# Addresses of the gated values and order of the passes in the second products of two feed-forwards

## The chip, the core and the metric

The kernel runs on one core of a Trainium2 chip. The metric is device time in microseconds (us), the median of several executions. Instructions run on TensorE (PE in the profile; its weight loads are listed apart as PEld), VectorE (DVE), ScalarE (ACT), GpSimd (POOL) and SyncE (SP, which issues DMAs). SBUF is the on-chip memory with 128 partitions; PSUM holds the results of matmuls in eight banks.

## The reference

One decoder layer on 512 tokens of width 1024, all in float32: a feed-forward, a token mixer and a second feed-forward, each between norms. The change is inside both feed-forwards, in the product with `w_out`:

```python
D_MODEL = 1024
SEQ = 512
D_FF = 2816

def rms_norm(x, g):
    xf = x.astype(jnp.float32)
    y = xf * lax.rsqrt(jnp.mean(xf * xf, axis=-1, keepdims=True) + EPS)
    return (y * g.astype(jnp.float32)).astype(x.dtype)

def swiglu_ffn(x, w_in, w_out):
    gate, up = jnp.split(x @ w_in, 2, axis=-1)
    return (jax.nn.silu(gate) * up) @ w_out

def reference(...):
    for l in range(DEPTH):
        x = x + 0.5 * rms_norm(swiglu_ffn(rms_norm(x, norm_pre[l, 0]), ffn1_w_in[l], ffn1_w_out[l]),
                               norm_post[l, 0])
        mixed = token_mixer(rms_norm(x, norm_pre[l, 1]), ...)
        x = x + rms_norm(mixed, norm_post[l, 1])
        x = x + 0.5 * rms_norm(swiglu_ffn(rms_norm(x, norm_pre[l, 2]), ffn2_w_in[l], ffn2_w_out[l]),
                               norm_post[l, 2])
    return x
```

`jax.nn.silu(gate) * up`, 512 tokens by 2816, are the gated values; their product with `w_out` (2816 by 1024) is the second product of a feed-forward.

## The kernel before

**Three passes.** Every large product is made of float32r matmuls. A float32 operand is kept as two parts: high, the value cast to float32r, and low, the rest. A product is three passes, high by high, high by low, low by high, summed in PSUM. Each matmul has its own weight load: 128 by 128 stationary values are loaded, then 256 columns of the moving operand stream past them.

**First products** (`prod`, L504 on, matmul at L520) multiply by `w_in`: weights stationary, the activations moving. They are written pass by pass: for one pass, eight matmuls (two halves of the output by four pieces of the sum), then the next pass. `p1` to `p7` and `c1` to `e4` are the names of the products of one step. `left` says which buffer a product's activations lie in: `xq` (four tiles) or `sq` (three). `p7` reads `sq[1]`, whose high and low parts lie at different offsets mod 128 elements. The first products of the head have copies of the weights in the `sq` buffers (`stay`).

**Second products** (`ffn_out`) multiply the gated values by `w_out`: the gated values are stationary, 128 tokens by 128, and the weights move, 256 columns of a tile `w` at a time. The 1024 columns are done in two halves of 512. In each half a loop goes over the eleven gated tiles `k2` (256 values of the 2816 each) in the order `OUT`; in the second half it goes over seven of them, and the last four tiles are left for `chunk`, which finishes one block of 128 tokens after the other so that the norm of a block (`post1`, `after`) can begin while the next is multiplied (`last`, L436 on). Four accumulators `C`, one PSUM bank each, hold the results: `C[i % 2][v]` for token block `i` and column quarter `v`.

Most tiles are plain (`plain`, matmul at L778): 48 matmuls for four token blocks, two column quarters, two pieces `kk` and three passes. The passes are the innermost loop, so that a matmul by the high part of a weight is followed by the same stationary values by its low part. The tiles in `QUARTERED` (four in the first half, three in the second) use seven products instead of eight of a 2 by 2 block product (`quartered` and `product`, matmul at L786): 42 matmuls. Their operands are quarters of the gated tile (`h_quarters`) and sums of them (`h_sums`), and four more accumulators `M` are turned into terms `T` by `common` and added to `C` by `add` (L754). The quarters `kept` in the first half are read again in the second.

**Where the operands lie.** The weights are split into high and low by ScalarE (cast, L220) and VectorE (subtraction, L222) into one of four slots of the tile `w`, each of 2048 elements. A slot is given back by `drop`, and the split of the next weight tile into it waits for the last matmul that reads it. The gated tiles are split by `two_parts` (L713 and L714) into buffers of tag `s` (three, shared with `sq`) or into the tiles `xq`, which are free by then. `s_place` and `x_place` choose the offset inside them: `NEXT` is 16 elements, 64 bytes, and the low part follows the high one by 1024 elements, in the sums of quarters by 1024 + 112. One buffer starts at byte 224 mod 512, a tile `xq` at 160, a slot of `w` at 480 (some slots of the mixer's weights at 416).

**What orders the work.** Most of the program is written in source order, and a scheduler orders each engine's queue when the kernel is built: it may put a ready instruction of lower priority ahead of one whose inputs come later. `more` makes gated tiles ahead of their use; `feed` splits weights ahead as far as slots are free. At the end of the first feed-forward `head4` begins the mixer's products (L475) with the slots that `chunk` gives back.

## Time and profile before

| What | Value |
|---|---|
| median of three runs | 958.07 us (958.02 to 958.52) |
| the profiled execution | 960.42 us |
| its span, first to last instruction | 958.7 us |
| mean granted clock of TensorE | 0.997 |
| second products of the first feed-forward | 225.7 to 349.5 us of the span |
| second products of the second feed-forward | 830.9 to 952.5 us of the span |
| matmuls at L520, L778, L786 | 3744, 1440, 588 |

The page gives for each engine its busy time, for each group of instructions (line, engine, operation, operands, shape, count) its busy time and the mean duration of one, then the idle time of the engine just before them. A matmul's duration of some 280 ns is longer than the distance between the starts of two, because they overlap in the array: the pitch from start to start is what adds up to time. The chain of waits follows the work that ended last back from the end; a row gives start, length, engine, line and count. The timeline merges neighbouring instructions of one line and one set of tiles into a row.

### The profile page before, as it was taken

The page shows a single profiled execution, that of the slowest core. Times are in us where ns is not written, and L with a number is a line of the kernel's source. Part 1 is how long each engine was busy: PE and PEld are TensorE (multiplying, and loading weights), DVE is VectorE, ACT ScalarE, POOL GpSimd, SP SyncE. Part 2 cuts the span into 40 slices and gives each one's busy share as a digit, 9 for nine tenths or more (in the row PEclk, how much of TensorE's full clock was granted, in tenths as well). Part 3 has the DMA queues.
Part 4 walks back from the last instruction along what each step waited for, and adds up shares of the span by engine and source line. Part 5 has one row for each costly group of instructions (what it writes and reads, how often), then busy time and mean ns, then how long its engine had stood idle before and what let it go on. Part 6 is the DMA issues. An engine that isn't in the chain of part 4 may idle for free.

```text
span 958.7 us, 18146 instructions
## 1 busy us (share of the span) xinstructions
PE 949.0 (99%) x7531; PEld 915.4 (95%) x7531; DVE 775.2 (81%) x1052; ACT 489.5 (51%) x691; POOL 119.1 (12%) x177
## 2 busy tenths in 40 slices
PE   9999999999999999999999999999999999999997
PEld 7999999999999999998887888899999999999997
DVE  6799989999788776688846565697998899977883
ACT  7645444455445456955622444664444444644541
POOL 2430000000001045200001210353000000000101
PEclk9999999999999999999999999999999999999999
DMA  9244343244232024421222124324334333224212
GB/s 320 77 134 130 116 128 111 89 133 131 87 96 84 23 78 123 111 66 44 70 64 67 45 80 139 112 67 133 111 110 121 111 110 101 66 89 133 73 39 88
DMA packets 81677, 96.13 MB, mean 100 GB/s; under 512 B 4117, under 2 KB 61497, under 8 KB 81594
## 3 DMA queue, kind: packets, MB, share of 16 engines
q1 hardware_dynamic: 81306, 94.44, 32.1%
q8 instruction: 59, 0.97, 0.4%
q10 hardware_dynamic: 288, 0.52, 0.2%
q14 instruction: 24, 0.20, 0.1%
HBM read 92.85 MB, written 2.10 MB: 99 GB/s over the span
## 4 chain that ended last, share of the span: by engine, by line
PE 62%; DVE 1%; ACT 0%; POOL 0%; issue 0%; POOLq 0%; DVEq 0%; ACTq 0%
PE ps L520 22%; PE ps L778 9%; PE ps L465 6%; PE ps L136 5%; PE ps L138 5%; PE ps L137 5%; PE ps L786 4%; PE ps L1163 2%; PE ps L475 1%; PE ps L295 1%; PE ps L1337 0%; PE ps L1248 0%; PE ps L1444 0%; PE ps L1417 0%; PE ps L1203 0%; PE ps L1441 0%
## 5 line engine op out<-in xcount | busy, mean ns | idle before, releaser
L220 ACT CAST w<-raw 128x1024 fp32r<-128x1024 f32 (+1 forms) x228 | 235.6, 1039 | 260.5 <-PE ps L520 94.5
L222 DVE TENSOR_TENSOR w<-raw,w 128x1024 fp32r<-128x1024 f32 (+1 forms) x228 | 281.9, 1243 | 46.9 <-ACT w L220 46.7
L520 PE MATMUL ps<-xq,w 128*128 128x256 f32 x2016 | 238.0, 277 | 0.0
L520 PEld LDWEIGHTS ps<-xq,w 128*128 128x128 f32 x2016 | 233.4, 188 | 0.0
L520 PE MATMUL ps<-sq,w 128*128 128x256 f32 x1440 | 171.0, 277 | 0.0
L520 PEld LDWEIGHTS ps<-sq,w 128*128 128x128 f32 x1440 | 167.4, 188 | 0.0
L778 PE MATMUL ps<-w,hs 128*128 128x256 f32 x1344 | 163.2, 281 | 0.0
L778 PEld LDWEIGHTS ps<-w,hs 128*128 128x128 f32 x1344 | 159.9, 189 | 0.3
L236 DVE TENSOR_TENSOR raw<-raw,raw 128x1024 f32<-128x1024 f32 x64 | 80.2, 1253 | 0.6
L136 PE MATMUL ps<-w,xq 128*128 128x512 f32 x192 | 79.0, 412 | 0.1
L138 PE MATMUL ps<-w,xq 128*128 128x512 f32 x192 | 75.0, 392 | 0.0
L137 PE MATMUL ps<-w,xq 128*128 128x512 f32 x192 | 74.9, 391 | 0.0
L383 POOL TENSOR_SCALAR col<-col 128x1 f32<-128x1 f32 x24 | 9.6, 401 | 500.9 <-ACT junk L382 500.8
L465 PE MATMUL ps<-xq,w 128*128 128x256 f32 x480 | 58.1, 283 | 0.0
L465 PEld LDWEIGHTS ps<-xq,w 128*128 128x128 f32 x480 | 56.9, 189 | 0.5 <-issue 0.5
L236 POOL TENSOR_TENSOR raw<-raw,raw 128x1024 f32<-128x1024 f32 x16 | 43.1, 2695 | 51.2 <-DVE w L222 42.0
L136 PEld LDWEIGHTS ps<-w,xq 128*128 128x128 f32 x192 | 36.1, 188 | 8.2 <-issue 0.8
L138 PEld LDWEIGHTS ps<-w,xq 128*128 128x128 f32 x192 | 36.1, 188 | 8.2 <-DVE xq L302 0.3
L137 PEld LDWEIGHTS ps<-w,xq 128*128 128x128 f32 x192 | 36.2, 189 | 6.7 <-issue 0.2
L713 ACT CAST hs<-hf 128x1024 fp32r<-128x1024 f32 x28 | 29.3, 1047 | 24.9 <-PE ps L786 24.9
L786 PE MATMUL ps<-w,hs 128*128 128x256 f32 x336 | 41.9, 282 | 0.0
L786 PEld LDWEIGHTS ps<-w,hs 128*128 128x128 f32 x336 | 40.6, 189 | 0.0
(251 smaller groups left out, 1151.8 us busy)
## 6 DMA issues: line engine op xcount, KB each, us to landing
raw<-in_ffn_w_in_dram SPq DMA_DIRECT2D x88, 512.0 KB, 3.8
raw<-in_ffn_w_out_dram SPq DMA_DIRECT2D x44, 512.0 KB, 4.0
raw<-in_w_mix_in_dram SPq DMA_DIRECT2D x28, 512.0 KB, 3.8
raw<-in_w_mix_out_dram SPq DMA_DIRECT2D x8, 512.0 KB, 3.9
out_dram<-xs SPq DMA_DIRECT2D x8, 256.0 KB, 2.1
xs<-in_x_dram SPq DMA_DIRECT2D x6, 256.0 KB, 6.8
gpost<-in_norm_post_dram SPq DMA_DIRECT2D x3, 512.0 KB
gpre<-in_norm_pre_dram SPq DMA_DIRECT2D x2, 512.0 KB, 4.1
```

What stands on the lines that cost most here:

```text
L136: mm(ps, sh, mh, start=start, stop=False, **kw)
L137: mm(ps, sh, ml, start=False, stop=False, **kw)
L138: mm(ps, sl, mh, start=False, stop=stop, **kw)
L220: nc.scalar.copy(hi, raw)
L222: nc.vector.tensor_tensor(lo, raw, hi.bitcast(F32), op=ALU.subtract)
L236: (nc.vector if late else nc.gpsimd).tensor_tensor(o, o, c, op=ALU.add)
L465: mm(ps[:, u0:u1], w[:, a, k, :], self.xop(k, b, u0, u1), start=k + n + m == 0, stop=k == ND - 1 and n == 2, skip_group_check=True,)
L520: self.nc.tensor.matmul(ps[:, c], wb[b][:, k, v], left[d][:, k, :], start=first and a + n + k == 0, stop=n == 2 and k == KH - 1, skip_grou ...
L713: self.nc.scalar.copy(hi, src)
L778: mm(out, a[kk][:, i * P : (i + 1) * P], w[:, b, kk, QUARTER * v : QUARTER * (v + 1)], start=begin and c == kk == n == 0, stop=kk == 1 and ...
L786: mm(ps[:, QUARTER * c : QUARTER * (c + 1)], A[a][:, c], B[b], start=begin and c == n == 0, stop=n == 2, skip_group_check=True,)
L1163: nc.tensor.matmul(sc[:, 64 * m : 64 * m + 64], k8[:, m], q8[:, m], start=True, stop=True)
```

## The change

Three things are altered, all in `ffn_out` and the helpers that place its operands.

The gated values of each feed-forward (`layer` 0 or 1) and each half of the columns get offsets of their own, in elements: (16, 0), (64, 64), (80, 80) and (96, 96) for the high and the low part, mod 128 elements, that is mod 512 bytes. With the buffers as they lie, the high and low parts start at bytes 288 and 224, 480 and 480, 32 and 32, 96 and 96 mod 512. The quarters kept from the first half stay where that half put them.

The matmuls of a plain tile are grouped: for two of the four token blocks, eight matmuls of the first pass, then eight of the second, then eight of the third; then the other two token blocks. Those of a quartered tile are grouped for each of its two weights: six and eight to a pass. In the last four tiles a group is one token block and one column quarter over all four tiles, eight matmuls to a pass.

The four weight slots of the last tiles are given back at the end of the last token block; the program between has no split.

```diff
-RAW, WBUF, PAD, LATE, NEAR, NEXT = 3, 4, 128, 112, 48, 16
+RAW, WBUF, PAD, LATE, NEAR = 3, 4, 128, 112, 48
...
+LIES = [[(16, 0), (64, 64)], [(80, 80), (96, 96)]]
...
-    def s_place(self, a=2, apart=False):
+    def s_place(self, lies, a=2):
 
         t = self.hpool.tile([P, 2 * D + PAD], F32R, tag="s", bufs=3, name=self.nm("hs"))
         part = lambda o: t[:, o : o + D].rearrange("p (k t) -> p k t", k=a)
-        return part(NEXT), part(D + (PAD if apart else NEXT))
-
-    def x_place(self, *n):
+        return part(lies[0]), part(lies[0] + D + (lies[1] - lies[0]) % PAD)
+
+    def x_place(self, lies, *n):
 
         out = []
         for m in range(2):
             t = self.xq[n[m % len(n)]].rearrange("p b k t -> p (b k t)")
-            o = 2 * NEXT + (D * m if len(n) == 1 else 0)
+            o = PAD - LATE + lies[m] + (D * m if len(n) == 1 else 0)
             out.append(t[:, o : min(o + D, 2 * D)])
         return out
...
+        def passes(group):
+
+            for n, (a, b) in enumerate(((0, 0), (0, 1), (1, 0))):
+                for out, left, right, first, last in group:
+                    mm(out, left[a], right[b], start=first and n == 0, stop=last and n == 2, skip_group_check=True)
 
         def plain(C, w, h, i, v, begin):
...
             for kk in range(2):
-                for n, (a, b) in enumerate(((hi, 0), (hi, 1), (lo, 0))):
-                    mm(
-                        out, a[kk][:, i * P : (i + 1) * P], w[:, b, kk, QUARTER * v : QUARTER * (v + 1)],
-                        start=begin and c == kk == n == 0, stop=kk == 1 and n == 2, skip_group_check=True,
-                    )
+                left = [t[kk][:, i * P : (i + 1) * P] for t in (hi, lo)]
+                right = [w[:, b, kk, QUARTER * v : QUARTER * (v + 1)] for b in range(2)]
+                yield out, left, right, begin and c == kk == 0, kk == 1
...
             w = self.pull()
-            product(M["p1"], A(1), quarter(w, 1), begin)
-            product(C[1][1], A(3), quarter(w, 3), False)
-            product(C[1][0], S(3), quarter(w, 2), False)
+            group = [*product(M["p1"], A(1), quarter(w, 1), begin), *product(C[1][1], A(3), quarter(w, 3), False)]
+            passes([*group, *product(C[1][0], S(3), quarter(w, 2), False)])
             self.drop(w)
             v = self.pull()
-            product(M["p7"], S(0), quarter(v, 0), begin)
-            product(M["p5"], S(1), quarter(v, 1), begin)
-            product(M["p6"], S(2), quarter(v, 2), begin)
-            product(C[0][1], A(2), quarter(v, 3), False)
+            group = [*product(M["p7"], S(0), quarter(v, 0), begin), *product(M["p5"], S(1), quarter(v, 1), begin)]
+            group += product(M["p6"], S(2), quarter(v, 2), begin)
+            passes([*group, *product(C[0][1], A(2), quarter(v, 3), False)])
             self.drop(v)
...
                     w = self.pull()
                     more(n + 3)
-                    for i in (0, 2, 1, 3):
-                        for v in range(2):
-                            plain(C, w, h, i, v, m == 0)
-                        if i > 1 and T and (half or m == PAIRS - 1):
-                            add(C, T, i % 2)
+                    for u in range(2):
+                        passes([mm for i in (u, u + 2) for v in range(2) for mm in plain(C, w, h, i, v, m == 0)])
+                        if T and (half or m == PAIRS - 1):
+                            add(C, T, u)
                     self.drop(w)
...
         def chunk(i):
             for v in range(2):
-                for w, h in zip(ws, hs):
-                    plain(C, w, h, i, v, False)
-                    if v and i == NT - 1:
-                        self.drop(w)
+                passes([mm for w, h in zip(ws, hs) for mm in plain(C, w, h, i, v, False)])
                 yield 2 - v
+            if i == NT - 1:
+                for w in ws:
+                    self.drop(w)
```

`product` now yields the same five values as `plain`, and `h_tile`, `h_quarters` and `h_sums` hand on the offsets of the half they are called for; `self.layer` counts the feed-forwards.

More of the change, by code (lines that the diff above doesn't have):

```diff
@@ L721, in h_tile, with h_quarters @@
         return hi, lo
-    def h_quarters(self, k2, n):
+    def h_quarters(self, k2, n, lies):
         src = self.by_chunk(k2)
-        parts = [v[:, : 3 * QUARTER].rearrange("p (k c t) -> p k c t", c=2, t=P) for v in self.x_place(n)]
+        parts = [v[:, : 3 * QUARTER].rearrange("p (k c t) -> p k c t", c=2, t=P) for v in self.x_place(lies, n)]
         self.two_parts(*(v[:, 0] for v in parts), src[:, 0, 1])
@@ L733, in by_chunk, with h_sums @@
         return self.hf[:, 2 * k2 : 2 * k2 + 2, :].rearrange("p k (c u t) -> p k u c t", u=2, t=P)
-    def h_sums(self, k2):
+    def h_sums(self, k2, lies):
         nc = self.nc
@@ L762, in more @@
                 half, k2 = seq[count[0]]
+                lies = LIES[self.layer][half]
                 count[0] += 1
@@ L765, in more @@
                     if half == 0:
-                        kept[k2] = self.h_quarters(k2, (1, 2, 0, 3)[QUARTERED[0].index(k2)])
-                    made.append((kept[k2], self.h_sums(k2)))
-                else:
-                    made.append((self.h_tile(k2, self.x_place(2, 3) if count[0] == len(seq) else None), None))
+                        kept[k2] = self.h_quarters(k2, (1, 2, 0, 3)[QUARTERED[0].index(k2)], lies)
+                    made.append((kept[k2], self.h_sums(k2, lies)))
+                else:
+                    made.append((self.h_tile(k2, self.x_place(lies, 2, 3) if count[0] == len(seq) else self.s_place(lies)), None))
+        def passes(group):
+            for n, (a, b) in enumerate(((0, 0), (0, 1), (1, 0))):
+                for out, left, right, first, last in group:
+                    mm(out, left[a], right[b], start=first and n == 0, stop=last and n == 2, skip_group_check=True)
         def plain(C, w, h, i, v, begin):
```

13 lines of the change are left out of this document (5 added, 8 removed).

## The prediction

> **What bounds the kernel.** I read the page first: busy times, groups, then the waits of the tensor engine.
>
> ```profile
> span 958.7 us, 18146 instructions
> PE 949.0 (99%) x7531; PEld 915.4 (95%) x7531; DVE 775.2 (81%) x1052; ACT 489.5 (51%) x691; POOL 119.1 (12%) x177
> L778 PE MATMUL ps<-w,hs 128*128 128x256 f32 x1344 | 163.2, 281 | 0.0
> L786 PE MATMUL ps<-w,hs 128*128 128x256 f32 x336 | 41.9, 282 | 0.0
> ```
>
> TensorE is busy 99% of the span, and the view of its waits adds up to 3.2 us, none of them at the changed lines L778 and L786. So the time there is the number of matmuls times their pitch (start to start), and nothing else ends last. The change keeps every matmul; only the pitch and the order can move the time. The granted clock is 0.997 over the run and 1.00 in these stages, so a pitch that differs is not the clock.
>
> The pitch shows in the chain of waits for the second feed-forward, whose columns are start, length, line and count:
>
> ```profile
> 830.88 5.65 PE ps L778 x48
> 836.53 2.74 PE ps L520 x24
> 839.27 5.65 PE ps L778 x48
> 844.92 4.95 PE ps L786 x42
> ...
> 933.14 18.93 PE ps L778 x167
> ```
>
> A plain block of 48 takes 5.65 us, 117.7 ns each; a quartered one 4.95/42 = 117.9. The 24 matmuls of L520 between them, of the same size, take 114.2, and 167 of the last matmuls of L778, in the same order as the slow ones, 113.4. So there are two paces, 113.3 and 117.8, and the second products run nearly all at the slow one: a matmul's start and the next weight load lock to each other in one of two ways.
>
> What selects the pace shows in the first products, by the timeline of TensorE (start, length, line, tiles, count):
>
> ```profile
> 630.69 2.99 PE L520 MATMUL ps<-xq,w 128*128 128x256 f32 x24
> 633.52 5.83 PE L520 MATMUL ps<-xq,sq 128*128 128x256 f32 x48
> 639.18 8.64 PE L520 MATMUL ps<-xq,w 128*128 128x256 f32 x72
> 647.66 2.99 PE L520 MATMUL ps<-xq,sq 128*128 128x256 f32 x24
> 650.49 2.99 PE L520 MATMUL ps<-xq,w 128*128 128x256 f32 x24
> 653.32 3.00 PE L520 MATMUL ps<-sq,w 128*128 128x256 f32 x24
> 656.15 2.88 PE L520 MATMUL ps<-xq,w 128*128 128x256 f32 x24
> 658.87 5.38 PE L520 MATMUL ps<-sq,w 128*128 128x256 f32 x46
> ```
>
> I divide the difference of starts by the count (a row's length has the last matmul's drain in it). Let the distance be the moving operand's start minus the start of the next stationary one, in bytes mod 512; the addresses are those of the built kernel before (w at 480, the buffers s at 224, xq at 160). With w stationary L520 has a distance of 192. Its rows at 630.69, 639.18 and 650.49 run at 117.8 to 117.9, the one at 656.15 and most that follow at 113.3, all in the same pass by pass order: so distance 192 bears both paces. The product between them, p7 at 653.32, has its low part at another address: passes of eight at 192, 192 (high part) and 256 (low part). In its records the eight at 256 are 120 apart, and after them the pace is the quick one. In every later p7 the eight at 256 average 117.6, the next eight 115.8, the next eight 113.3, so p7 means 115.5. Distance 448 (xq moving, sq stationary) also bears both paces: 113.3 from 621.8 to 624.3, 117.8 at 647.66. Where the low part of the stationary makes it 256 inside those products, eight matmuls run at a flat 120, in four places. Distance 384 occurs at a few: once each time L520 hands over to L778, where the matmul takes 117 to 118, the next few 114 to 119, and the pace is slow from there (four of four), and in four matmuls of L1248 (118, 120, 119, 118; its load is 100 wide). Distance 0 occurs only as the single matmul ahead of each L520 behind L778: 117, then 121 and 122. So I take odd multiples of 64 (192, 448) as bearing either pace, and even ones (0, 256, 384) as held at about 120.
>
> **Part by part.** Each feed-forward has 504 matmuls in the first half of the columns (7 plain blocks of 48, 4 quartered of 42), 318 in the loop of the second (4 and 3), and 192 in its last four tiles. Before, all gated parts are at distance 192, but for the low sums at 256. After:
>
> 1. First feed-forward, first half, (16, 0): 192 for passes one and two, 256 for pass three, eight and eight and eight: p7's pattern. 504 x (115.5 - 117.8) = -1.2 us. Bounds: 113.3 throughout, -2.3; never kicked to the quick pace, (2 x 117.8 + 120)/3 = 118.5, +0.4. I take p7's row, the nearest.
> 2. First feed-forward, second half, (64, 64): distance 0. In the loop 192 plain and 72 with sums, 264 in all, go from 117.8 to 120: +0.6; the 54 that read the quarters kept from the first half stay, 0. The last tiles now average 114.6 (186 records, without six with stalls), so 186 x (120 - 114.6) = +1.0. Together +1.6. Bounds: at 113.3, -1.4; at 125, the highest single pitch at a change of distance, +3.8.
> 3. Second feed-forward, first half, (80, 80): 448, either pace, entered from L520 through a single matmul at 128, which no row shows; the nearest, 384, led to the slow pace each time. So 0; at 113.3 it is -2.3; at most +0.1.
> 4. Second feed-forward, second half, (96, 96): 384. Loop 264 x 2.2 = +0.6; the last tiles lose the quick pace: 167 x (120 - 113.4) = +1.1, the other 25 +0.1. Together +1.7. Bounds -1.3 and +3.9.
> 5. The order of the last tiles. Before, each of the four weights runs its three passes before the next; after, pass one asks for the high parts of all four pairs within eight matmuls. The timeline of the first feed-forward shows when they come:
>
> ```profile
> 325.43 1.05 ACT L220 CAST w<-raw 128x1024 fp32r<-128x1024 f32 x1 [4.30 <-PE ps L778]
> 326.38 1.04 ACT L713 CAST hs<-hf 128x1024 fp32r<-128x1024 f32 x1
> 327.98 1.22 DVE L714 TENSOR_TENSOR hs<-hf,hs 128x1024 fp32r<-128x1024 f32 x1
> ```
>
> The third gated tile's high part is there at 327.42. Matmul 5 of the first tile would want it at 325.3 + 4 x 0.12 = 325.8: 1.6 us, with all of TensorE's queue behind it, and behind that the norm of tile 0. But the trace already has other outputs' matmuls ahead of the waiting ones (the second column quarter starts at 326.74, before the first is done), and stalls only 0.17 us there. With 28 matmuls of other outputs to put ahead I take 0.2 each, 0.4 for both; bounds 0 and 3.2. Elsewhere grouping asks for low parts later than before.
> 6. A weight slot of the last tiles is read up to matmul 18 of the last 24 instead of 6, to 348.7. The first cast into it starts at 348.43 because ScalarE is at L301 until 348.55; so it comes 0.3 us later. What the next matmuls wait for is VectorE's L222 at 351.00, behind four operations that need no slot: 0, and 0.3 if that cover went.
> 7. p5 and p7 end some ten matmuls later within the block, near 319.4; their first reader, L754 at 319.66, is behind VectorE's L222 until then: 0. The casts, subtractions and loads are the same in number and queue; no DMA moves.
>
> Sum: -1.2 + 1.6 + 0 + 1.7 + 0.4 = +2.5 us. The profiled execution took 960.42 (span 958.7), so 962.9 in its terms; it lies 2.35 above the median 958.07, so the forecast is **960.6**.
>
> **Rivals.** A, the other side: the order by pass itself brings the quick pace in every stage. For it, the long quick stretch of the first products is ordered so; against it, the rows from 630.69 to 653.32 are ordered so and slow, and the old order is quick at 933.14. It gives 504 x 4.5 twice, 318 x 4.5 twice, and 0.3 in the last tiles: -7.7, so 950.4. It decides once the even distances (0 and 384) hold under 116.
> B: as forecast, but (80, 80) locks to the quick pace: -2.3, 958.3. For it the stretch at 621.8; against it, all four times L520 went from a slow 192 to 448 it stayed slow.
> C: distance 0, where both streams start alike in all three passes, holds 125: +2.2 beyond the sum, 962.8. For it, 125 is seen once; against it, it is one matmul at a change.
> D: the matmuls put ahead in the last tiles do not cover the wait: 3.2 instead of 0.4, 963.4. Against it, the stalls of 0.17.
> E: neither address nor order decides the pitch; it is set by how TensorE enters a stage, and the entries stay: 958.1. Against it, the flat 120 at 256. The Trainium skill, "TensorE: Matmul & The Clock Gate", section "Step-by-step: what each phase is for", says that weight loads have an SBUF read port of their own and take no read bandwidth from the running matmul; by that rule E holds, but the pitches of 113.3 and 120 at one size and one clock do not agree with it.
>
> **How the numbers follow.** Forecast 36%, A 20%, B 17%, C 12%, D 8%, E 7%. A measurement of this kernel tells 0.2%, 1.9 us, from no change. Slower by more (over 960.0): 28 of the forecast's 36, C and D: 48%. Within: 8 of the forecast, 13 of B, E: 28%. Faster: A and 4 of B: 24%. The forecast's own range is 959 to 962. The range over the cases, 952.5 to 964.0, leaves out most of A (its bound is 950.4) and the ends of C and D.
>
> **What would show it.** Right: the first block rows of the second feed-forward's second half over 118.5, its last tiles no longer at 113.4, the first half of the first near 115.5. Step 3 is told by one chain row of L786: 4.95 (slow) or 4.76 (quick). Step 5 by pitches over 160 at the head of the last tiles. Wrong: a plain block of 5.44 us at distance 0 or 384 (then A), or all at 5.65 (then E).

## The result, and the profile after

The changed kernel takes 960.88 us, median of seven runs (960.01 to 962.52), against 958.02 (957.70 to 959.91) for the kernel before beside it: a ratio of 1.0027, with a 95% interval of 1.0016 to 1.0039. So it is slower, by an amount just above what can be told from no change. The profiled execution took 960.88 us too.

The page of the changed kernel, its span, the busy times and the groups of the changed matmuls, which now all stand at L779:

```profile
span 959.1 us, 18156 instructions
PE 949.7 (99%) x7531; PEld 915.6 (95%) x7531; DVE 775.9 (81%) x1052; ACT 489.7 (51%) x691; POOL 118.6 (12%) x177
L779 PE MATMUL ps<-w,hs 128*128 128x256 f32 x1680 | 222.1, 282 | 0.0
L779 PE MATMUL ps<-w,xq 128*128 128x256 f32 x348 | 62.7, 281 | 0.0
```

TensorE is as busy as before, and nothing waits at L779 for long. The durations of one matmul (281 and 282 ns) are those of before, so the page alone can't show what changed; the time from stage to stage can.

The profile of before was not a good yardstick, as its own time of 960.42 us against a median of 958.07 had hinted. The unchanged kernel was therefore profiled a second time (experiment 1 below): 958.79 us, span 957.1. The windows below cut each of the two traces at the first matmul of each stage: first half of the columns, loop of the second half, last four tiles, for the first and then the second feed-forward. Columns: the window, its length, busy time and instructions of each engine, the granted clock, the DMA share and GB/s. First the second profile of the kernel before:

```profile
225.90:288.00 62.10, 62.10 (x530) 62.10 (x529) 51.17 (x79) 28.16 (x37) 0.26 (x2) 1.00 0.32 97
288.00:325.51 37.51, 37.51 (x320) 37.44 (x319) 32.94 (x49) 20.58 (x31) 3.10 (x7) 1.00 0.21 67
325.51:349.96 24.45, 24.45 (x209) 24.33 (x209) 15.62 (x26) 12.60 (x34) 7.51 (x19) 1.00 0.01 2
828.34:890.43 62.09, 62.09 (x530) 62.09 (x529) 51.17 (x79) 28.15 (x37) 0.25 (x2) 1.00 0.32 97
890.43:927.95 37.52, 37.52 (x321) 37.45 (x319) 32.96 (x49) 20.58 (x31) 3.10 (x7) 1.00 0.21 67
927.95:950.90 22.95, 22.95 (x193) 22.66 (x192) 11.02 (x18) 5.32 (x16) 3.77 (x10) 1.00 0.19 70
```

And the same six stages of the changed kernel:

```profile
225.82:288.22 62.40, 62.40 (x530) 62.40 (x529) 51.70 (x80) 28.15 (x37) 0.28 (x2) 1.00 0.31 97
288.22:326.26 38.04, 38.04 (x320) 38.04 (x319) 33.22 (x48) 20.56 (x31) 3.03 (x7) 1.00 0.20 65
326.26:352.03 25.77, 25.32 (x210) 24.85 (x208) 16.27 (x28) 12.69 (x34) 7.41 (x19) 1.00 0.01 2
829.93:892.03 62.10, 62.10 (x531) 62.10 (x529) 51.65 (x80) 28.16 (x37) 0.26 (x2) 1.00 0.31 97
892.03:929.56 37.53, 37.53 (x320) 37.53 (x319) 33.10 (x48) 20.57 (x31) 3.08 (x7) 1.00 0.19 66
929.56:952.95 23.39, 23.39 (x194) 22.98 (x192) 10.98 (x18) 5.32 (x16) 3.50 (x10) 1.00 0.19 69
```

The second column is what to compare: +0.30, +0.53, +1.32 in the first feed-forward, then +0.01, +0.01, +0.44 in the second. The 1.32 is 0.5 of pitch, 0.2 of stalls at the head of the last tiles, and 0.6 that the first matmul of the head waits (step 6 of the prediction). Of it 0.50 comes back at once in the head that follows (14.29 us from the end of that window to the first matmul of the next line, against 14.79). The sum is +2.1 us, and the spans differ by 2.0: the ledger closes, and everything lies in the changed stages. The granted clock is 1.00 in every row.

Where the 2.35 us of the first profile of before came from shows in two windows behind the last tiles of its first feed-forward, the head and the L465 stretch that follows. The first two rows are the first profile, its mean granted clock in the third column from the right:

```profile
349.46:365.84 16.38, 14.76 (x112) 14.57 (x113) 11.81 (x17) 6.73 (x14) 6.29 (x7) 0.90 0.74 195
365.84:430.90 65.06, 65.06 (x555) 64.58 (x554) 48.87 (x72) 48.38 (x57) 16.25 (x34) 1.00 0.33 90
```

And the second profile of the same kernel:

```profile
349.96:364.75 14.79, 13.29 (x114) 13.09 (x113) 11.70 (x16) 6.67 (x13) 6.27 (x7) 1.00 0.75 202
364.75:428.50 63.75, 63.75 (x555) 63.27 (x554) 49.43 (x72) 48.28 (x57) 16.39 (x35) 1.00 0.35 95
```

In the first execution the granted clock averaged 0.90 in the head. It was 0.50 for 3.4 us of it, and from its first matmul (at 349.55 and 349.96) the head took 1.5 us more:

```profile
352.62:356.00 3.38, 3.38 (x19) 3.38 (x18) 2.99 (x5) 1.00 (x3) 1.60 (x3) 0.50 0.75 195
```

The first 288 matmuls of L465 behind it ran at the slow pace instead of the quick one, 117.8 ns against 113.3 (+1.3), in the same order and at the same addresses. Their row in the chains of the first and the second profile, and in that of order_only (experiment 2), where the line is L467 and the pace slow once more:

```profile
366.01 33.92 PE ps L465 x288
364.92 32.64 PE ps L465 x288
364.35 33.92 PE ps L467 x288
```

In the other twelve traces of this document they run at 113.3. Against the slow head and the slow L465, the last tiles of the first execution were quicker: 114.6 and 113.8 ns from start to start without the stalls, where the second execution has 117.0 and 117.5.

From the chain of waits in the changed kernel, the first block of the first feed-forward, then the second feed-forward, against the rows of before:

```profile
225.98 5.69 PE ps L779 x48
830.09 5.65 PE ps L779 x48
835.74 2.74 PE ps L523 x24
838.48 114.49 PE ps L779 x966
```

The first block of the second feed-forward still takes 5.65 us, 117.7 ns each (distance 448, slow). All the rest, 966 matmuls, averages 118.5. In the first feed-forward the same block takes 5.69: 118.5 each, two passes at 117.8 and one at 120.

### The profile page after: what moved, and what is told of

Read it like the earlier page. It is cut to its first block, busy times and chain, and to the rows that moved or that the text cites. A ratio compares the mean times of both kernels' runs of the same rounds, so it can differ in the third digit from the quotient of the medians.

```text
span 959.1 us, 18156 instructions
## 1 busy us (share of the span) xinstructions
PE 949.7 (99%) x7531; PEld 915.6 (95%) x7531; DVE 775.9 (81%) x1052; ACT 489.7 (51%) x691; POOL 118.6 (12%) x177
## 4 chain that ended last, share of the span: by engine, by line
PE 98%; POOL 0%; ACT 0%; DVE 0%; issue 0%; DVEq 0%; POOLq 0%; ACTq 0%
PE ps L523 45%; PE ps L779 25%; PE ps L467 6%; PE ps L138 5%; PE ps L140 5%; PE ps L139 5%; PE ps L1164 2%; PE ps L297 1%; PE ps L477 1%; PE ps L1338 0%; PE ps L1249 0%; PE ps L127 0%; PE ps L134 0%; PE ps L1445 0%; PE ps L1418 0%; PE ps L1204 0%
## 5 line engine op out<-in xcount | busy, mean ns | idle before, releaser
L523 PE MATMUL ps<-xq,w 128*128 128x256 f32 x2016 | 237.9, 277 | 0.0
L523 PEld LDWEIGHTS ps<-xq,w 128*128 128x128 f32 x2016 | 233.4, 188 | 0.0
L779 PE MATMUL ps<-w,hs 128*128 128x256 f32 x1680 | 222.1, 282 | 0.0
L779 PEld LDWEIGHTS ps<-w,hs 128*128 128x128 f32 x1680 | 209.0, 190 | 0.5 <-ACT hs L716 0.2
L523 PE MATMUL ps<-sq,w 128*128 128x256 f32 x1440 | 171.0, 277 | 0.0
L523 PEld LDWEIGHTS ps<-sq,w 128*128 128x128 f32 x1440 | 167.4, 188 | 0.0
L779 PE MATMUL ps<-w,xq 128*128 128x256 f32 x348 | 62.7, 281 | 0.0
L467 PE MATMUL ps<-xq,w 128*128 128x256 f32 x480 | 56.8, 279 | 0.0
L467 PEld LDWEIGHTS ps<-xq,w 128*128 128x128 f32 x480 | 55.6, 188 | 0.5 <-issue 0.5
L779 PEld LDWEIGHTS ps<-w,xq 128*128 128x128 f32 x348 | 50.6, 190 | 0.0
L138 PEld LDWEIGHTS ps<-w,xq 128*128 128x128 f32 x192 | 36.1, 188 | 8.3 <-issue 0.8
L140 PEld LDWEIGHTS ps<-w,xq 128*128 128x128 f32 x192 | 36.0, 188 | 8.2 <-DVE xq L304 0.3
L139 PEld LDWEIGHTS ps<-w,xq 128*128 128x128 f32 x192 | 36.2, 188 | 6.7 <-issue 0.2
```

The lines of the kernel that those rows point to most:

```text
L138: mm(ps, sh, mh, start=start, stop=False, **kw)
L139: mm(ps, sh, ml, start=False, stop=False, **kw)
L140: mm(ps, sl, mh, start=False, stop=stop, **kw)
L467: mm(ps[:, u0:u1], w[:, a, k, :], self.xop(k, b, u0, u1), start=k + n + m == 0, stop=k == ND - 1 and n == 2, skip_group_check=True,)
L523: self.nc.tensor.matmul(ps[:, c], wb[b][:, k, v], left[d][:, k, :], start=first and a + n + k == 0, stop=n == 2 and k == KH - 1, skip_grou ...
L779: mm(out, left[a], right[b], start=first and n == 0, stop=last and n == 2, skip_group_check=True)
```

## The experiments

Distance is used as in the prediction: start of the moving operand minus start of the next stationary one, in bytes mod 512. Stage times are those of windows cut as above, in the order first half, loop, last tiles; pitches are from the records of single matmuls. All ratios are against the kernel before on the same chip.

### 1. before_again: the kernel before, unchanged

> The kernel before, unchanged, profiled a second time, since its profiled execution took 960.42 us and its median is 958.0. Theory 1 (executions differ by which of two paces long stretches of equal matmuls lock into): in an execution of about 958 us some stretch outside the second products runs at 113.3 ns a matmul that ran at 117.8 in the first profile; the candidate is the 480 matmuls of L465 (58.1 us busy before, 56.8 in the changed kernel), so 56 us there and a span of 956.5. The second products stay at 117.7 to 117.9 in both loops and near 114 in the last tiles. Rival (the profile was slow for another reason, spread over all): every group some 0.25% shorter, L465 at 58.0.

958.79 us, span 957.1. The rows are shown above. First halves and loops repeat to 0.01 us (62.10 and 37.5, as in the first profile). The last tiles do not repeat: of 191 pitches, 134 and 170 were under 115.6 ns in the first profile's two feed-forwards, 35 and 13 in the second. Which pace the last tiles fall into is a matter of the single execution, and the prediction had read it from one. In the records of both traces the pace there changes only behind a gap between matmuls or behind the shorter matmuls of L295: in the second feed-forward it goes from 117.8 to 113.3 behind a pitch of 214 ns in the first profile, and from 113.3 to 117.8 behind pitches of 163 and 226 in the second, with the distance at 192 throughout. Of what was expected, the quick L465 came (56.8 us busy against 58.1), and last tiles near 114 did not; the fall of the clock was in neither theory.

### 2. order_only: the new order, the old addresses

```diff
-LIES = [[(16, 0), (64, 64)], [(80, 80), (96, 96)]]
+LIES = [[(16, 16), (16, 16)], [(16, 16), (16, 16)]]
...
-        hi, lo = self.s_place(lies, 4)
+        hi, lo = self.s_place((16, 0), 4)
```

> Order of the changed kernel, addresses of the one before (distance 192, low sums at 256). Theory 1 (the distance decides, the order does not): the loops stay at 117.8 ns as in both kernels at a distance of 192; the last tiles can lock quick again because their distance is odd times 64, and have at their head the stalls of the grouped order, 0.5 us each: ratio 1.000 to 1.001. Rival (the order by pass is what costs): ratio 1.003 like the changed kernel, with 120 ns in the last tiles.

958.59 us, ratio 1.0006 (0.9997 to 1.0015). Stages 62.14, 37.50, 24.88 and 62.15, 37.49, 22.49. The order by pass brings no other pace where the distance stays 192: rival A falls. What it costs is at the head of the last tiles. There the pitches over 140 ns add up to 0.61 and 0.47 us above the others, against 0.40 and 0.23 in experiment 1.

### 3. addr_only: the new addresses, the old order

`plain`, `product`, `quartered`, `chunk` and the loop are those of before the change; shown is the loop:

```diff
-                    for u in range(2):
-                        passes([mm for i in (u, u + 2) for v in range(2) for mm in plain(C, w, h, i, v, m == 0)])
-                        if T and (half or m == PAIRS - 1):
-                            add(C, T, u)
+                    for i in (0, 2, 1, 3):
+                        for v in range(2):
+                            plain(C, w, h, i, v, m == 0)
+                        if i > 1 and T and (half or m == PAIRS - 1):
+                            add(C, T, i % 2)
```

> Addresses of the changed kernel, order of the one before (passes innermost). Theory 1: distance 0 holds 120 ns in the second half of the first feed-forward and in its last tiles, 384 holds 118 to 119 in those of the second, 448 stays at 117.8: with no added stalls at the head of the last tiles, ratio 1.002 (1.5 to 2.5 us more). Rival (the order costs): ratio 1.000, last tiles near 114.

959.62 us, ratio 1.0012 (1.0003 to 1.0021). Stages 62.09, 38.04, 24.95 and 62.10, 37.57, 23.11. The loop at distance 0 costs its +0.53 in either order, so that part belongs to the address alone. The first half of the first feed-forward does not: with single matmuls at 256 between pairs at 192 it stays at 62.09, and only groups of eight at 256 make it 62.40.

### 4. tail_old: the changed kernel with the last tiles in the old order

```diff
-                passes([mm for w, h in zip(ws, hs) for mm in plain(C, w, h, i, v, False)])
+                for w, h in zip(ws, hs):
+                    for mm3 in plain(C, w, h, i, v, False):
+                        passes([mm3])
+                    if v and i == NT - 1:
+                        self.drop(w)
                 yield 2 - v
-            if i == NT - 1:
-                for w in ws:
-                    self.drop(w)
```

> The changed kernel with the old order in the last four tiles of each feed-forward alone. Theory 1: the pitch of the last tiles stays at 120 and 119, since their addresses stay; only the stalls at their head go back to those of before, 0.2 to 0.5 us a feed-forward: ratio to before 1.002. Rival (the grouped order of the last tiles carries the loss): ratio 1.000.

960.08 us, ratio 1.0021 (1.0011 to 1.0030). Last tiles 24.96 and 23.16 us instead of 25.77 and 23.39; the pitches over 140 ns now add up to 0.35 and 0.21 us above the others, against 0.59 and 0.46 in the changed kernel. So the order of the last tiles costs about half a microsecond in stalls, as step 5 had it, and the rest of what they lost is the pitch: 119.9 and 118.7 in either order. The stall shows in the timeline of the changed kernel, columns as before:

```profile
327.42 1.05 ACT L716 CAST hs<-hf 128x1024 fp32r<-128x1024 f32 x1
328.52 0.30 PEld L779 LDWEIGHTS ps<-w,hs 128*128 128x128 f32 x2 [0.23 <-ACT hs L716]
```

The weight load that wants the third gated tile's high part waits 0.23 us for ScalarE's cast of it. It comes at 328.52, some 19 matmuls into the stage, and not at matmul 5, because the matmuls of other outputs stand ahead of it.

### 5. swap: the two feed-forwards change addresses

```diff
-LIES = [[(16, 0), (64, 64)], [(80, 80), (96, 96)]]
+LIES = [[(80, 80), (96, 96)], [(16, 0), (64, 64)]]
```

> The changed kernel with the two feed-forwards' addresses exchanged: (80, 80) and (96, 96) in the first, (16, 0) and (64, 64) in the second. Theory 1 (the distance decides, not the place in the program): first half of the first feed-forward 117.8 ns, second half of the first 118.0 in the loop and 118 to 119 in the last tiles, first half of the second 118.4, second half of the second 119.6 in the loop and 120 in the last tiles; ratio near that of the changed kernel, 1.002 to 1.003. Rival (the entry into each stage decides): the pitches stay where they were, 118.4, 119.6, 117.8, 118.0 in that order.

961.84 us, ratio 1.0029 (1.0019 to 1.0040). The first halves and loops of this kernel:

```profile
225.61:287.71 62.10, 62.10 (x531) 62.10 (x529) 51.66 (x80) 28.16 (x37) 0.26 (x2) 1.00 0.32 97
287.71:325.25 37.54, 37.54 (x321) 37.54 (x319) 33.10 (x48) 20.58 (x31) 3.08 (x7) 1.00 0.20 67
828.66:891.06 62.40, 62.40 (x530) 62.40 (x529) 51.70 (x80) 28.15 (x37) 0.28 (x2) 1.00 0.31 96
891.06:929.10 38.04, 38.04 (x320) 38.04 (x319) 33.22 (x48) 20.56 (x31) 3.03 (x7) 1.00 0.22 66
```

The four stage times change places with the addresses to 0.01 us. So these stage times follow the address, and not the feed-forward, its data, or how TensorE enters it: rival E falls for these distances. At distance 192 it is partly right, for there the pace depends on what ran before, as L465 showed and the next runs show. One address of the stationary operand for another is worth 0.5 us in 318 matmuls here. The Trainium skill, "TensorE: Matmul & The Clock Gate", section "Step-by-step: what each phase is for", says that loading the next weights takes no read bandwidth from the running matmul. Read, as in the prediction, to mean that the address can't cost time, it does not agree with these rows. By what path the address acts, no run shows.

### 6. kick: the kernel before with one weight tile 64 bytes lower

All gated values are at distance 192, and the order is that of before. One slot of `w` can lie 64 bytes lower. It is given to the weights of the second and third gated tile of the first half, wherever these fall into that slot:

```diff
-            n, late = next(f for f in fit if not f[1] or (it.key[0] == "mix" and b == 512))
+            out1 = it.key[1] == "out" and it.key[2] == 0 and it.key[3] in (1, 2)
+            n, late = next(f for f in fit if not f[1] or (it.key[0] == "mix" and b == 512) or (out1 and f[0] == 0))
...
-        hi, lo = self.s_place(4, True)
+        hi, lo = self.s_place(4)
```

In the first feed-forward this puts 18 matmuls at distance 128, in the second 48.

> The kernel before with its order, the low sums at 64 bytes as all else (distance 192 everywhere), and one weight tile early in the first half of each feed-forward 64 bytes lower, so that its 18 or 48 matmuls have an even distance, 128, made by the moving operand. Theory 1 (a spell at an even distance that ends by a change of the moving operand's address leaves the quick pace, as behind every p7 and at each L520 after L778, and distance 192 then keeps it): after that tile 113.3 ns in both halves of both feed-forwards, some 1450 matmuls at 4.45 ns less, 6.4 us: ratio 0.993 to 0.994. Rival (in the second products the pace cannot be changed by the weights' address, or order by pass is needed to hold it): 117.8 throughout, ratio 1.000.

955.95 us, ratio 0.9977 (0.9967 to 0.9987). Rows of TensorE's timeline around the 18, where the shifted tile is the first 18 matmuls from 239.18 on (L779 is a plain tile here, L787 a quartered one):

```profile
233.53 5.81 PE L779 MATMUL ps<-w,hs 128*128 128x256 f32 x48
239.18 1.61 PE L787 MATMUL ps<-w,xq 128*128 128x256 f32 x12
240.62 2.94 PE L787 MATMUL ps<-w,hs 128*128 128x256 f32 x24
243.40 0.84 PE L787 MATMUL ps<-w,xq 128*128 128x256 f32 x6
244.08 5.60 PE L779 MATMUL ps<-w,hs 128*128 128x256 f32 x48
249.52 1.52 PE L787 MATMUL ps<-w,xq 128*128 128x256 f32 x12
```

Start to start: (239.18 - 233.53)/48 = 117.7 ns ahead of the 18, (240.62 - 239.18)/12 = 120 in them, (249.52 - 244.08)/48 = 113.3 behind them, where the addresses are again those of the first row. The pace stays at 113.3 to the end of the loop: 60.43 and 36.50 us. Of the 36.50, 36.0 are the 318 pitches; the rest is a gap behind the last of them, where TensorE now comes early and waits for VectorE (0.30 us, L755). So distance 192 holds whichever pace it is given, and a stretch of other addresses can change it over.

The second feed-forward, with its 48, ran at 117.8 behind them (62.14 and 37.51), so half of the theory failed: the ratio is not its 0.993 to 0.994. The two stretches differ in more than their length. The 18 are met at 117.8; the 48 stand directly behind 24 matmuls of L521 that end at 113.3. The 18 average 120.3 ns, in threes of 118, 120 and 122; the 48 average 118.5, in fives of about 115, 117, 122, 120 and 119.

### 7. kick_pass: the same in the new order

The changed kernel with all gated values at (16, 16), the last tiles as in tail_old, and the shifted weight tiles of kick.

> As the run kick, but with the matmuls of the loops grouped pass by pass as in the change (the last tiles in the old order). Theory 1: the order does not matter to the pace, 113.3 ns after the shifted tile: ratio 0.993 to 0.994, as kick. Rival (only the grouped order holds the quick pace): kick at 1.000 and this one at 0.993.

954.75 us, ratio 0.9960 (0.9948 to 0.9973). First halves 60.42 and 62.13, loops 36.39 and 37.45: as kick, so the order by pass neither helps nor hinders the change of pace. The last tiles of its profile average 115.3 ns in the first feed-forward (the quick pace of its loop is lost behind the gap at the end of it, comes back behind another some 33 matmuls later, and is lost again behind the matmuls of L298) and 113.4 in the second, whose loop ran at 117.8.

### 8. spell18_pass: 18 matmuls at distance 128 in both feed-forwards

As kick_pass, with the shifted tile chosen so that it gives 18 matmuls in both:

```diff
-            out1 = it.key[1] == "out" and it.key[2] == 0 and it.key[3] in (1, 2)
+            out1 = it.key[1] == "out" and it.key[2] == 0 and it.key[3] == {"f1": 2, "f2": 4}[it.key[0]]
```

> The matmuls grouped by pass as in kick_pass, all gated values at distance 192; the 64 byte shift is moved to the weight tile of the third gated tile in the first feed-forward and of the fifth in the second, so that each feed-forward has one stretch of exactly 18 matmuls at distance 128 with distance 192 ahead of it and after it. Theory, the length of the stretch decides (18 led to 113.3 ns in kick and kick_pass, 48 did not): both feed-forwards run at 113.3 from the stretch on; first half of the first 60.4 to 60.8 us, of the second 60.6 to 61.2 against 62.1, second half's loop 36.0 to 36.6 in both; ratio 0.993 to 0.995, about 952.5. Rival, something of the second feed-forward other than the length keeps it at 117.8: 62.1 and 37.5 there, ratio 0.996, about 954.7.

952.93 us, ratio 0.9950 (0.9938 to 0.9963): the theory's numbers. Windows of the first halves and loops:

```profile
225.84:286.26 60.42, 60.42 (x530) 60.42 (x529) 51.24 (x79) 28.18 (x37) 0.19 (x1) 1.00 0.33 99
286.26:322.65 36.39, 36.21 (x320) 36.04 (x319) 33.15 (x49) 20.80 (x32) 3.38 (x7) 1.00 0.22 71
825.54:886.36 60.82, 60.82 (x530) 60.82 (x529) 51.33 (x79) 28.18 (x37) 0.19 (x1) 1.00 0.32 98
886.36:922.75 36.39, 36.21 (x321) 36.04 (x319) 33.14 (x49) 20.79 (x32) 3.38 (x7) 1.00 0.23 71
```

Behind the 18 both feed-forwards run at 113.3 to the end of the loop; the 36.39 hold a gap of 0.35 there, as in kick. So the second feed-forward takes the quick pace too. That the length decides is not shown by this, because the move of the tile also changed how the stretch is met: at 117.8, as in the first feed-forward, and no longer right behind L524's quick matmuls. This version beats both kernels with the same matmuls, two of its weight tiles 64 bytes lower.

### 9. spell18_24: a second stretch, met at the quick pace

kick, with the shifted tiles of the third and the fifth gated tile in both feed-forwards:

```diff
-            out1 = it.key[1] == "out" and it.key[2] == 0 and it.key[3] in (1, 2)
+            out1 = it.key[1] == "out" and it.key[2] == 0 and it.key[3] in (2, 4)
```

> The old order of the matmuls, all gated values at distance 192, and the 64 byte shift on the weight tiles of the third and the fifth gated tile in both feed-forwards: in the first, 18 matmuls at distance 128, then 90 at 192, then 24 at 128, then 192; in the second, one stretch of 18 as in spell18_pass. Theory (the length decides, and the state ahead does too): the second feed-forward goes to 113.3 after its 18, 60.6 to 61.2 for its first half and 36.0 to 36.6 for the loop after it; in the first the 24 run at 120 and the pace after them is open: 113.3 if a stretch that ends on the quick side is kept, 60.4 to 60.8, or 117.8 if only some lengths lead to the quick pace, 61.7. Ratio 0.992 to 0.996. Rival, the place and not the length decides: second feed-forward 62.1 and 37.5.

956.00 us, ratio 0.9980 (0.9971 to 0.9989). The chain of the second feed-forward, whose 18 begin the second row of 42:

```profile
835.65 5.65 PE ps L779 x48
841.30 4.95 PE ps L787 x42
846.25 5.65 PE ps L779 x48
851.90 4.90 PE ps L787 x42
856.80 5.44 PE ps L779 x48
862.24 4.76 PE ps L787 x42
```

5.65 becomes 5.44 and 4.95 becomes 4.76, on either side of the one shifted tile, late in the stage and in the old order: the 18 do it in both places that were tried. In the first feed-forward the 18 led to 113.3, and the 24 that came 90 matmuls later, met at the quick pace, led back to 117.8, where it stayed: 61.78 and 37.52 us, so the ratio lies above the 0.992 to 0.996 expected. A stretch at 128 can undo what another has done. The 24 ran at 118.7, in the fives of kick's 48, and not at the 120 expected.

### 10. moving_part: the distance alternates by the moving operand

As kick_pass, but only the high part of a shifted weight tile is 64 bytes lower, so that passes one and three are at 128 and pass two at 192:

```diff
-            w = self.wt[:, o : o + 2 * D].rearrange("p (b k t) -> p b k t", b=2, k=a)
+            if late and it.key[1] == "out":
+                w = self.wt[:, o : o + 2 * D + 32].rearrange("p (b x) -> p b x", b=2)[:, :, :D]
+                w = w.rearrange("p b (k t) -> p b k t", k=a)
```

> As kick_pass, but only the high part of the shifted weight tiles is moved by 64 bytes: the moving operand then alternates pass by pass, in groups of 6 or 8, between distance 128 (passes one and three) and 192 (pass two). In the changed kernel's first half of the first feed-forward it was the stationary operand whose address alternated in groups of 6 or 8, and it stayed at 117.8 throughout. Theory, what differs from p7 is which operand moves, or how often: the distance changed by the moving operand leads to 113.3 after one such tile: first feed-forward 60.4 to 60.8 us in the first half. Rival, stretches of 6 and 8 are too short and only some lengths do it: 62.1 to 62.2 in both, the time within 0.1% of before with the second feed-forward as in kick_pass.

952.96 us, ratio 0.9952 (0.9936 to 0.9967). The two first halves:

```profile
225.13:285.52 60.39, 60.39 (x530) 60.39 (x529) 51.25 (x79) 28.17 (x37) 0.19 (x1) 1.00 0.33 99
824.52:884.88 60.36, 60.36 (x530) 60.36 (x529) 51.19 (x79) 28.17 (x37) 0.19 (x1) 1.00 0.31 99
```

In the first feed-forward six matmuls at 128 take 120.8 ns each, and the six at 192 behind them average 116 and end at 113.5; behind the next six at 128 the pace is 113.3 to the end. The second feed-forward goes over as well, with the tile whose 48 at 128 had left it at 117.8 in kick_pass: here its stretches at 128 are of 8, 16 and 8, with eights at 192 between them. So the place of that tile doesn't bar the quick pace. The theory's number came, but the next run took its reason away.

### 11. stat128: the distance alternates by the stationary operand, at 128

The changed kernel with first halves at (16, 32) and (32, 16), so that groups of eight alternate between 192 and 128 where the changed kernel's had 192 and 256; second halves at 192:

```diff
-LIES = [[(16, 0), (64, 64)], [(80, 80), (96, 96)]]
+LIES = [[(16, 32), (16, 16)], [(32, 16), (16, 16)]]
...
+        if lies[1] < lies[0]:
+            return part(lies[0] + D), part(lies[1])
         return part(lies[0]), part(lies[0] + D + (lies[1] - lies[0]) % PAD)
```

> The changed kernel with its first halves at (16, 32) in the first feed-forward and (32, 16) in the second: the stationary address alternates pass by pass between distances 192, 192, 128 and 128, 128, 192, in groups of 6 or 8, as the moving address did in moving_part; both second halves stay at 192 throughout. Theory, alternating by the stationary operand never leads to the quick pace (as at (16, 0) in the changed kernel): both first halves stay at 117.8 where the distance is 192 and near 120 where it is 128, mean 118.3 to 118.6 in the first feed-forward (62.1 to 62.5 us) and 118.8 to 119.3 in the second (62.2 to 62.7), loops 37.5. Rival, the distance of 128 and not the operand made the difference to (16, 0): 113.3 soon after the first groups at 128, then mixed paces, mean 114.5 to 117, first halves 57.7 to 59.0 between the first and last start, that is 60.3 to 61.7 us.

955.69 us, ratio 0.9971 (0.9961 to 0.9980): the rival was right (the second feed-forward's 61.76 lies just above its 61.7).

```profile
225.91:287.08 61.17, 61.17 (x531) 61.17 (x530) 51.43 (x80) 28.18 (x37) 0.19 (x1) 1.00 0.32 98
826.99:888.75 61.76, 61.76 (x531) 61.76 (x529) 51.60 (x80) 28.18 (x37) 0.22 (x2) 1.00 0.31 97
```

In its records the first eight at 128 lead from 117.7 to 114.8 in the sixteen at 192 behind them, and from the fourth tile on the groups of the plain tiles run at 117.8 (128) and 114.5 (192) all through that first half, most of each sixteen at 113. It is the distance of 128, not which operand makes it, that separates this from the changed kernel's (16, 0). In the loops, where only the kept quarters alternate, stretches of two at 128 changed the pace over each time: six times from quick to slow, three times back.

### 12. quick_16_0: the changed kernel's (16, 0), entered at the quick pace

spell18_pass with its second halves at (16, 0):

```diff
-LIES = [[(16, 16), (16, 16)], [(16, 16), (16, 16)]]
+LIES = [[(16, 16), (16, 0)], [(16, 16), (16, 0)]]
```

> spell18_pass with the second halves of both feed-forwards at the changed kernel's (16, 0): TensorE comes into them at the quick pace, then the stationary address alternates, sixteen matmuls at 192 and eight at 256. Theory, an alternation by the stationary operand does not keep the quick pace: the loops go to 117.8 and 120 within the first block, 37.0 to 37.8 us against 36.4 in spell18_pass, ratio 0.996 to 0.999. Rival, what I predicted of p7: after each eight at 256 the pace goes back to 113.3, mean near 115.5, loops 36.5 to 37.0, ratio 0.994 to 0.996.

955.75 us, ratio 0.9968 (0.9957 to 0.9979). The two loops:

```profile
286.09:323.62 37.53, 37.53 (x320) 37.53 (x319) 33.23 (x49) 20.57 (x31) 3.36 (x7) 1.00 0.21 68
887.33:924.86 37.53, 37.53 (x320) 37.53 (x319) 33.23 (x49) 20.57 (x31) 3.36 (x7) 1.00 0.21 68
```

36.39 in spell18_pass, the gap of 0.35 at its end included, and 37.53 here without one. The first sixteen run at 113.4, the eight at 256 behind them at 119.5, the next sixteen at 117.8, and the quick pace does not come back. So (16, 0) not only fails to lead to the quick pace, it loses it.

## Why the prediction came out as it did

The forecast of 960.6 us is near the 960.9 measured. Its sum of +2.5 us compares with +2.1 stage by stage against the second profile of before, and with +2.9 between the medians; no profile lies at the median of before, so the other 0.8 us is not placed. But the terms are not all right, and that the total came so near is in good part luck: step 1 was 1.5 us too low, the loop of step 4 and the two pitches of the last tiles together 2.1 us too high. By its steps, rounded (the prediction adds its step 4 up to +1.7):

| Step | Forecast, us | Measured, us |
|---|---|---|
| 1: first half of the first, (16, 0) | -1.2 | +0.30 |
| 2: loop at distance 0 | +0.6 | +0.53 |
| 2: last tiles, pitch | +1.0 | +0.5 |
| 3: first half of the second, 448 | 0 | 0.01 |
| 4: loop at distance 384 | +0.6 | +0.01 |
| 4: last tiles, pitch | +1.2 | +0.2 |
| 5: stalls of the last tiles, both | +0.4 | +0.4 |
| 6: weight slots | 0 | +0.1 |

**Step 1 failed.** It took p7's row of the first products as the pattern of (16, 0) because both alternate 192, 192 and 256 in groups of eight. The runs show that the pattern doesn't carry over. In every trace p7's 20 eights at 256 end on the quick pace, the 18 that are met at it and the two that are met at the slow one: the next eight average 115.6 to 116.9 ns, those behind them 113.3. In the changed kernel all 16 groups of eight at 256 that lie between stretches at 192 in the second products end on the slow pace, and in quick_16_0 both that are met at the quick one lose it. The bound "never kicked to the quick pace", +0.4, was the case, and the stage came to +0.30. A nearer row stood in the profile of before. In the four places from which the prediction read its flat 120, between stretches at 448, the eights at 256 are made by the stationary operand, as at (16, 0); one lies in the row at 633.52 that it shows. Behind all four the pace is 117.8, and so it is in all 14 traces, 56 of 56, one of them met at 113.3 (before_again, at 30.10 us). Read for what follows it, that row gives the +0.4 of the bound. Why the two kinds of stretch at 256 end differently is open: they differ in the operand that makes the distance and in both addresses. For 128, stat128 shows that the operand is not what decides; a stretch at 256 made by the moving operand inside the second products was not tried.

**Step 2** was right in the loop (120.0 flat at distance 0, as read from the eights at 256), and rival C's 125 did not come. In the last tiles the pitch of 119.8 came as forecast, but what it replaced was read from the one profile of before.

**Step 3** was right: 448, entered from L523, kept the slow pace; rival B fell. **Step 4** failed in the loop: distance 384 is not held at 120. Its plain blocks average 118.5 to 118.7, and the groups of the quartered tiles, mixed with quarters kept at 448, average between 114 and 121, so that the stage costs nothing. In the last tiles the pitch averages 118.6 instead of 120.

**The last tiles of steps 2 and 4** were mis-sized for a second reason: before's pace there is not fixed (114.6 and 113.8 in one execution, 117.0 and 117.5 in another). Against the first profile the pitch cost 191 x 5.2 ns = +1.0 and 191 x 4.8 = +0.9, near the forecast's +1.0 and +1.2. The same execution carried 2.8 us elsewhere (the fall of the clock in the head, 1.5, which no other trace has, and the slow L465, 1.3, which only order_only's has), and the subtraction of 2.35 at the end took this away in one lump. The forecast treated the offset as a constant; that it lay in stages which the change does not touch was not looked up, and the rows for it were there.

**Step 5** was sized right: stalls of 0.59 and 0.46 us against 0.40 and 0.23, tail_old takes them away again, and rival D's 3.2 did not come. **Step 6** held: the first matmul of the head now waits 0.42 us for the cast into the later slot, and the wait for VectorE behind it shrinks from 1.50 to 0.93 in all; from the last matmul ahead of the head to the first behind it, 0.1 us remains. **Step 7** shows nothing. Rival A fell with order_only, and rival E, for the distances of the changed kernel, with swap.

That a matmul's start and the next weight load "lock to each other" is not shown as a mechanism. In the profile the next load starts 2 to 5 ns behind the start of a matmul at either pace; what differs is the mean length of the loads and matmuls: 188 and 276 ns at 113.3, 189 to 190 and 281 to 282 at 117.8 (before, from 940 to 945 and from 845 to 849 us), 192 and 283 at 120 (the changed kernel, from 289 to 293 us).

## What to carry to other kernels

Where one engine is busy 99% of the span, the pitch from start to start is the quantity to read, stage by stage, because busy shares don't show it and the mean duration of a group, which mixes its stages, shows it faintly. Profile the unchanged kernel twice before forecasting a change of 0.3%: a stage whose pace differs between two executions of one kernel can't be a term with one value, and a profile that lies off the median should be taken apart before its offset is subtracted. And a pattern read from one pair of operands is a guess for another pair; here the cheap test, moving one buffer by 64 bytes, told more than the reading.

## What the runs showed of the hardware

- Float32r matmuls of 256 columns, each with its own weight load, keep one of three pitches over long stretches at a granted clock of 1.00: 113.3, 117.8 or 120.0 ns. Which of them depends on the distance mod 512 bytes and, at distance 192, also on what ran before. Distance 0 is flat at 120.0. Two distances have no single pitch: 384 wanders around 118.5, and 128 averages 120.3 in the stretches of 18 and 118.5 to 118.7 in those of 48 and 24.
- At distance 192 the pace is kept while the matmuls follow each other: 318 in a row at 113.3 or at 117.8 with the same addresses and order. Behind a gap or other matmuls it can change, even from one execution of a kernel to the next: the last tiles and the first 288 matmuls of L465 are the two cases. In long stretches at 448 of the second products only the slow pace was seen.
- Stretches at distance 128, the shortest of two matmuls, can change it over. A stretch of 18, met at the slow pace, led to the quick one in all eight cases (one each in kick and kick_pass, two each in spell18_pass, spell18_24 and quick_16_0). The one stretch of 24, met at the quick pace, led to the slow one. Behind the two of 48, which follow quick matmuls of the first products, the pace was slow. Length and the pace ahead were changed together in these runs, so which of them decides the side on which a stretch ends is open. The pace ahead alone does not: in stat128 the pitch is back at 113 a few matmuls behind eights that are met at it, and 117.8 behind twos that are met at it.
- So 64 bytes in the place of one weight tile, for 18 matmuls of each feed-forward, were worth 0.5% of this kernel (ratio 0.9950).
